# A log-sum-exp kernel: its second pass as a section with its own semaphores on the ScalarE queue, SyncE out of the branch, and a smaller sample in the range test

## The chip, the cores and the metric

The kernel runs on one core of a Trainium2 chip. The metric is the time of one execution in microseconds (us), lower is better. The profile's span, from the first to the last recorded instruction, is about 1.8 us shorter than that time in most kernels here. Engines: ACT is ScalarE, DVE is VectorE, SP is SyncE, PE is TensorE, POOL is GpSimd. A "q" after the name means the engine's sequencer (waits, branches, register loads and DMA issues, which are not counted as busy).

## The reference

The input x is 32 x 512 x 1024 float32, normally distributed: 67 MB to read, 64 KB to write.

```python
max_x = np.max(x, axis=-1, keepdims=True)
return max_x.squeeze(-1) + np.log(np.sum(np.exp(x - max_x), axis=-1))
```

## The kernel before

The first pass takes no maximum. It loads rows, takes Exp and sums, then Log. A test then decides whether every sum was in a safe range. Only if not does a second, stable pass run. On normally distributed inputs it never runs, so what matters here is what the test and the skipped branch cost.

```python
loads = ["R8 R8", "R8 R8", "R8 R8", "R7 R6 A A", ..., "T2", "T1", "A", "A"]   # 17 loads, on SyncE
ENGINES = [SP, Activation, DVE]
# ... first pass: load -> Exp on ScalarE -> sum on VectorE (R, T) or ScalarE (A) ...
nc.scalar.activation(out=res[:, EARLY:NC], in_=sumexp[:, EARLY:NC], func=AF.Ln)       # L121
nc.sync.dma_start(out=out_view, in_=res)                                              # L122

# range test: sums clamped to [1e-15, 1e15] must equal themselves (L127, L131); the last
# row is tested by the maximum of a sample of its elements (L136, L137); PE counts (L135-L141)
nc.vector.reduce_max(out=bad[:, 2:3], in_=last_row[:, 0, 0 : d // 4], axis=AX.X)      # L136
nc.vector.tensor_scalar(out=bad[:, 1:2], in0=bad[:, 2:3], scalar1=LOG_LOW, ...)       # L137
# ... three matmuls into count ...
nc.vector.tensor_scalar(out=fine, in0=count, scalar1=HIGH, scalar2=None, op0=ALU.is_lt)  # L143
all_fine = nc.values_load(fine[0:1, 0:1], engines=ENGINES, ...)                       # L144
with tc.If(all_fine < 1, preferred_fallthrough_block=False):                          # L148
    # ... second pass: loads on SyncE, max, subtract, Exp, sum, Log, store on SyncE ...
```

The framework tracks its semaphores by counting. An engine that skips the branch therefore first bumps the semaphores that the skipped instructions would have bumped. For SyncE these are four DMA semaphores.

## Time and profile before

| | value |
|---|---|
| time, median of 6 runs | 165.31 us (165.22 to 165.62) |
| DMA engines busy, 20 to 155 us | 99 to 100%, 420 to 429 GB/s |
| VectorE / ScalarE busy | 122.2 / 116.8 us |
| from the end of the last VectorE sum to the end of the span ("the tail") | 4.01 us |

The table by stages of the kernel before; its columns are the stage, its length, busy time (and count) of PE, PEld, DVE, ACT and POOL, then the granted clock, the share of the DMA engines, and GB/s.

```profile
0.00:20.00 20.00, 0.00 (x0) 0.00 (x0) 0.09 (x2) 1.28 (x1) 0.20 (x4) 1.00 0.98 410
20.00:60.00 40.00, 0.00 (x0) 0.00 (x0) 27.86 (x4) 27.90 (x4) 0.00 (x0) 1.00 0.99 424
...
140.00:155.00 15.00, 0.00 (x0) 0.00 (x0) 13.27 (x15) 14.96 (x16) 0.00 (x0) 1.00 1.00 420
155.00:161.10 6.10, 0.19 (x2) 0.09 (x2) 5.94 (x12) 5.85 (x9) 0.00 (x0) 1.00 0.56 224
161.10:164.10 3.00, 0.24 (x4) 0.14 (x4) 0.30 (x2) 0.03 (x1) 0.00 (x0) 1.00 0.10 27
```

Up to 155 us the kernel is bound by its loads. In the last 3 us no engine computes for more than a tenth of the time; what lasts there is waits and sequencer work. The timeline of the kernel before shows the way to the flag (start, duration, engine, line):

```profile
159.99 0.09 DVE L104 DVE_READ_ACCUMULATOR ring<-ring 128x1 f32 x1
...
160.66 0.41 DVE L136 TENSOR_REDUCE bad<-ring 128x1 f32<-128x256 f32 x1
...
161.15 0.35 SPq L122 DMA_DIRECT2D out_dram<-res  x1
...
161.60 0.14 DVE L143 TENSOR_SCALAR fine<-count 1x1 int32<-1x1 f32 x1 [0.33 <-PE count L141]
```

The records by source line show what the sequencers do after the flag (engine, operation, count, duration in ns as minimum/median/maximum, first and last start in us). L144 is the load of the flag, L148 the branch, L186 the closing of the program:

```profile
L144 SPq TENSOR_LOAD <-fine x1: 462/462/462, 161.8 to 161.8; - x1
L144 ACTq TENSOR_LOAD <-fine x1: 469/469/469, 161.8 to 161.8; - x1
L144 DVEq TENSOR_LOAD <-fine x1: 543/543/543, 161.8 to 161.8; - x1
...
L148 SPq EVENT_SEMAPHORE  x4: 17/17/17, 162.4 to 162.6; - x4
L148 SPq COMPARE_BRANCH  x2: 38/44/49, 162.3 to 162.7; - x2
...
L186 SPq EVENT_SEMAPHORE  x9: 17/28/28, 162.9 to 164.0; - x9
L186 SPq DRAIN  x3: 7/7/7, 163.3 to 163.6; - x3
L186 DVEq DRAIN  x2: 10/30/50, 163.2 to 163.7; - x2
```

All three engines load the flag at 161.8. SyncE then has a compare, four bumps and a jump (the profile calls both branch forms COMPARE_BRANCH), and after that a list of closing waits for the program's semaphores. Its drain is later than VectorE's, and the closing barrier, which POOL gathers, waits for the last of them.

### The profile page before, as it was taken

To read this page: it belongs to the slowest core of one execution; us is meant where nothing else is said; L and a number is where in the kernel's file an instruction comes from. 1 tells how busy PE (TensorE), PEld (TensorE's weight loads), DVE (VectorE), ACT (ScalarE), POOL (GpSimd) and SP (SyncE) were. 2 spreads that over 40 slices of the span, in tenths; PEclk is the share of its full clock that TensorE was granted. 3 is DMA by queue.
4 is the path that set the end of the run, shared out by engine and by line. 5 is a ranking of instruction groups with operands and counts; after the bars stand their busy time and mean duration, and the time that the engine had idled before them with its cause. 6 is when DMAs were issued, how large, how long until landed. Compare 5 with 4: busy or idle time off the path is not lost.

```text
span 164.1 us, 205 instructions
## 1 busy us (share of the span) xinstructions
PE 0.4 (0%) x6; PEld 0.2 (0%) x6; DVE 122.2 (74%) x44; ACT 116.8 (71%) x53; POOL 0.2 (0%) x4
## 2 busy tenths in 40 slices
PE   0000000000000000000000000000000000000001
PEld 0000000000000000000000000000000000000000
DVE  0000000699959999399999995999998999979893
ACT  3000039990699708995399929999969599999992
POOL 0000000000000000000000000000000000000000
DMA  7979998997997999899999989999999999999960
GB/s 256 511 335 431 511 399 367 511 463 304 511 431 335 511 450 404 374 464 479 433 447 419 433 365 449 419 432 440 417 439 415 433 425 419 415 421 423 409 248 20
DMA packets 2594, 67.19 MB, mean 409 GB/s; under 512 B 288, under 2 KB 416, under 8 KB 800
## 3 DMA queue, kind: packets, MB, share of 16 engines
q1 hardware_dynamic: 2592, 67.18, 95.7%
q14 instruction: 2, 0.02, 0.0%
HBM read 67.11 MB, written 0.07 MB: 409 GB/s over the span
## 4 chain that ended last, share of the span: by engine, by line
DMA 64%; DVE 22%; ACT 11%; issue 1%; SPq 0%; PE 0%; DVEq 0%
DMA ring<-in_x_dram 64%; DVE sumexp L99 20%; ACT ring L92 11%; DVE ring L104 1%; SPq L72 0%; DVE bad L136 0%; DVE clamped L127 0%; PE count L140 0%; DVE bad L137 0%; DVE clamped L131 0%; DVE fine L143 0%; PE count L141 0%; DVEq L127 0%
## 5 line engine op out<-in xcount | busy, mean ns | idle before, releaser
L99 DVE TENSOR_REDUCE sumexp<-ring 128x8 f32<-128x8192 f32 (+7 forms) x20 | 116.2, 5854 | 38.2 <-ACT ring L92 38.2
L92 ACT ACTIVATE ring<-ring 128x8192 f32<-128x8192 f32 (+7 forms) x24 | 101.7, 4283 | 43.6 <-DMA ring<-in_x_dram 43.6
L90 ACT ACTIVATE ring<-ring 128x1024 f32<-128x1024 f32 x12 | 12.5, 1039 | 0.0
L104 DVE SCALAR_TENSOR_TENSOR ring<-ring 128x512 f32<-128x512 f32 x8 | 5.1, 684 | 0.0
L90 ACT ACTIVATION_READ_ACCUMULATOR ring<-ring 128x1 f32 x12 | 2.2, 186 | 0.0
L67 ACT ACT_TABLE_LOAD x1 | 1.3, 1283 | 0.7 <-PEq L175 0.7
L90 ACT ACTIVATE last_exp<-ring 128x1024 f32<-128x1024 f32 x1 | 1.0, 1005 | 0.0
L68 DVE MEMSET ones<- 128x1 f32 x1 | 0.1, 59 | 0.8 <-PEq L175 0.8
L104 DVE DVE_READ_ACCUMULATOR ring<-ring 128x1 f32 x8 | 0.7, 82 | 0.0
L135 PE MATMUL count<-far,bad 128*1 128x1 f32 x2 | 0.2, 164 | 160.8 <-DVE clamped L131 160.8
L136 DVE TENSOR_REDUCE bad<-ring 128x1 f32<-128x256 f32 x1 | 0.4, 415 | 0.0
L143 DVE TENSOR_SCALAR fine<-count 1x1 int32<-1x1 f32 x1 | 0.1, 145 | 0.3 <-PE count L141 0.3
L131 DVE SCALAR_TENSOR_TENSOR clamped<-clamped,sumexp 128x127 f32<-128x127 f32 x1 | 0.3, 290 | 0.0
L127 DVE TENSOR_SCALAR clamped<-sumexp 128x127 f32<-128x127 f32 x1 | 0.2, 227 | 0.1
L135 PEld LDWEIGHTS count<-far,bad 128*1 128x1 f32 x2 | 0.1, 80 | 160.8 <-DVE clamped L131 160.8
L119 ACT ACTIVATE res<-sumexp 128x104 f32<-128x104 f32 x1 | 0.3, 273 | 0.0
L121 ACT ACTIVATE res<-sumexp 128x24 f32<-128x24 f32 x1 | 0.2, 222 | 0.0
L140 PE MATMUL count<-far,bad 128*1 128x1 f32 x2 | 0.2, 164 | 0.3 <-DVE bad L137 0.3
L141 PE MATMUL count<-ones,sumexp 128*1 128x1 f32 x2 | 0.2, 164 | 0.0
L90 ACT ACTIVATION_READ_ACCUMULATOR last_exp<-ring 128x1 f32 x1 | 0.2, 185 | 0.0
L137 DVE TENSOR_SCALAR bad<-bad 128x1 f32<-128x1 f32 x1 | 0.2, 154 | 0.0
L141 PEld LDWEIGHTS count<-ones,sumexp 128*1 128x1 f32 x2 | 0.1, 82 | 0.0
(7 smaller groups left out, 0.6 us busy)
## 6 DMA issues: line engine op xcount, KB each, us to landing
ring<-in_x_dram SPq DMA_DIRECT2D x1, 7680.0 KB, 33.1
ring<-in_x_dram SPq DMA_DIRECT2D x1, 7168.0 KB, 30.7
ring<-in_x_dram SPq DMA_DIRECT2D x1, 5120.0 KB, 31.4
ring<-in_x_dram SPq DMA_DIRECT2D x1, 4608.0 KB, 33.7
ring<-in_x_dram SPq DMA_DIRECT2D x1, 4096.0 KB, 29.4
ring<-in_x_dram SPq DMA_DIRECT2D x2, 2048.0 KB, 32.7
ring<-in_x_dram SPq DMA_DIRECT2D x1, 3072.0 KB, 36.3
ring<-in_x_dram SPq DMA_DIRECT2D x2, 1024.0 KB, 38.8
```

The lines of the kernel that those rows point to most:

```text
L67: nc.scalar.preload_act_table_set("natural_log_exp_and_others")
L90: exp = nc.scalar.activation(out=o, in_=v, func=AF.Exp, accum_out=sums)
L92: exp = nc.scalar.activation(out=v, in_=v, func=AF.Exp)
L99: added = [nc.vector.reduce_sum(out=sums, in_=v, axis=AX.X)]
L104: nc.vector.scalar_tensor_tensor(out=lo, in0=lo, scalar=1.0, in1=ring[:, p + r, H:d], op0=ALU.mult, op1=ALU.add, accum_out=sums[:, r : r + 1],
L119: nc.scalar.activation(out=res[:, 0:EARLY], in_=sumexp[:, 0:EARLY], func=AF.Ln)
L121: nc.scalar.activation(out=res[:, EARLY:NC], in_=sumexp[:, EARLY:NC], func=AF.Ln)
L127: nc.vector.tensor_scalar(out=clamped[:, 0:LAST], in0=sumexp[:, 0:LAST], scalar1=LOW, scalar2=HIGH, op0=ALU.max, op1=ALU.min,)
L131: nc.vector.scalar_tensor_tensor(out=clamped[:, 0:LAST], in0=clamped[:, 0:LAST], scalar=0.0, in1=sumexp[:, 0:LAST], op0=ALU.bypass, op1=AL ...
L135: nc.tensor.matmul(count, lhsT=bad[:, 0:1], rhs=far, start=True, stop=False)
L136: nc.vector.reduce_max(out=bad[:, 2:3], in_=last_row[:, 0, 0 : d // 4], axis=AX.X)
L141: nc.tensor.matmul(count, lhsT=sumexp[:, LAST:NC], rhs=ones, start=False, stop=True)
```

## The change

It means to shorten that ending. The second pass becomes a critical section with two semaphores of its own, so that the framework has no bumps of DMA semaphores to make up for when the section is skipped. Its loads and store move to the ScalarE queue, and SyncE neither loads the flag nor branches. The sample of the last row shrinks from 256 to 64 elements.

```diff
-    ENGINES = [mybir.EngineType.SP, mybir.EngineType.Activation, mybir.EngineType.DVE]
+    ENGINES = [mybir.EngineType.Activation, mybir.EngineType.DVE]
...
-    nc.vector.reduce_max(out=bad[:, 2:3], in_=last_row[:, 0, 0 : d // 4], axis=AX.X)
+    nc.vector.reduce_max(out=bad[:, 2:3], in_=last_row[:, 0, 0 : d // 16], axis=AX.X)
...
     with tc.If(all_fine < 1, preferred_fallthrough_block=False):
-        for c0 in range(0, NC, RING):
-            ...
-            load(0, c0, s)
-            nc.vector.tensor_reduce(out=neg, in_=v, op=ALU.max, axis=AX.X, negate=True)
-            ...
-        nc.sync.dma_start(out=out_view, in_=res)
+        with tc.tile_critical(sync_engine=mybir.EngineType.Activation):
+            with nc.semaphore("landed") as landed, nc.semaphore("ready") as ready:
+                for c0 in range(0, NC, RING):
+                    ...
+                    nc.scalar.dma_start(out=v, in_=x_rows[:, c0 : c0 + s, :]).then_inc(landed, 16)
+                    nc.vector.wait_ge(landed, rows)
+                    nc.vector.tensor_reduce(...).then_inc(ready, 1)
+                    ... (the same steps, each waiting on and bumping these two) ...
+                nc.scalar.dma_start(out=out_view, in_=res).then_inc(landed, 16)
+                nc.scalar.wait_ge(landed, rows + 16)
```

More of the change, by code (lines that the diff above doesn't have):

```diff
@@ L148 @@
     with tc.If(all_fine < 1, preferred_fallthrough_block=False):
-        for c0 in range(0, NC, RING):
-            s = min(RING, NC - c0)
-            v = ring[:, 0:s, :]
-            neg = clamped[:, c0 : c0 + s]
-            load(0, c0, s)
-            nc.vector.tensor_reduce(out=neg, in_=v, op=ALU.max, axis=AX.X, negate=True)
-            nc.vector.tensor_add(out=v, in0=v, in1=neg[:, :, None].to_broadcast([P, s, d]))
-            nc.scalar.activation(out=v, in_=v, func=AF.Exp)
-            nc.vector.reduce_sum(out=sumexp[:, c0 : c0 + s], in_=v, axis=AX.X)
@@ L158 @@
-        nc.scalar.activation(out=res, in_=sumexp, func=AF.Ln)
-        nc.vector.tensor_sub(out=res, in0=res, in1=clamped)
-        nc.sync.dma_start(out=out_view, in_=res)
+        with tc.tile_critical(sync_engine=mybir.EngineType.Activation):
+            with nc.semaphore("landed") as landed, nc.semaphore("ready") as ready:
+                rows = 0
+                steps = 0
+                for c0 in range(0, NC, RING):
+                    s = min(RING, NC - c0)
+                    v = ring[:, 0:s, :]
+                    neg = clamped[:, c0 : c0 + s]
+                    if c0:
+                        nc.scalar.wait_ge(ready, steps)
+                    nc.scalar.dma_start(out=v, in_=x_rows[:, c0 : c0 + s, :]).then_inc(landed, 16)
+                    rows += 16
+                    nc.vector.wait_ge(landed, rows)
+                    nc.vector.tensor_reduce(
+                        out=neg, in_=v, op=ALU.max, axis=AX.X, negate=True
+                    ).then_inc(ready, 1)
+                    nc.vector.wait_ge(ready, steps + 1)
+                    nc.vector.tensor_add(
+                        out=v, in0=v, in1=neg[:, :, None].to_broadcast([P, s, d])
+                    ).then_inc(ready, 1)
+                    nc.scalar.wait_ge(ready, steps + 2)
+                    nc.scalar.activation(out=v, in_=v, func=AF.Exp).then_inc(ready, 1)
+                    nc.vector.wait_ge(ready, steps + 3)
+                    nc.vector.reduce_sum(
+                        out=sumexp[:, c0 : c0 + s], in_=v, axis=AX.X
+                    ).then_inc(ready, 1)
+                    steps += 4
+                nc.scalar.wait_ge(ready, steps)
+                nc.scalar.activation(out=res, in_=sumexp, func=AF.Ln).then_inc(ready, 1)
+                nc.vector.wait_ge(ready, steps + 1)
+                nc.vector.tensor_sub(out=res, in0=res, in1=clamped).then_inc(ready, 1)
+                nc.scalar.wait_ge(ready, steps + 2)
+                nc.scalar.dma_start(out=out_view, in_=res).then_inc(landed, 16)
+                nc.scalar.wait_ge(landed, rows + 16)
```

## The prediction

> **What bounds the kernel.** Loads. In the table by stages the DMA engines are 98 to 100% busy from 0 to 155 us, at 410 to 429 GB/s; VectorE (122.2 us) and ScalarE (116.8 us) are not full. The chain of waits is 64% load, 22% VectorE, 11% ScalarE up to about 160 us. The order listing shows no differing load, Exp or sum, so only the last 4 us can move.
>
> **The tail before** (timeline; records by line, sequencers included). The 256-element maximum (L136) runs 160.66 to 161.08, then the threshold 161.11, matmuls 161.32, `fine` 161.60 to 161.74. SyncE, ScalarE and VectorE load `fine` at 161.77 to 161.78 (462, 469, 543 ns). SyncE then compares and branches (162.30), does four semaphore bumps (162.40 to 162.63) and a jump (162.70), and begins its closing waits at 162.87, about 65 ns apart: seven, then two drains, the last at 163.39. VectorE's closing drain is at 163.17, ScalarE's at 162.87, so SyncE comes last. The output DMA was issued at 161.15 and landed at 162.70: by 162.87 that wait was over. The closing barrier lasts to 164.09. The Trainium skill ("Advanced Engine Details and Errata", Control Flow Timing) gives about 108 ns to a compare-and-branch; here SyncE's record is 49 ns, with 100 ns from its start to the next instruction.
>
> **What the change does.**
> 1. Takes SyncE's load of `fine`, compare, four bumps and jump (161.77 to 162.87) off its path. It goes straight to the closing waits; the output's landing (162.70, second wait) then holds it. After this come four waits and two drains, about 0.38 us, so the last drain is near 163.1 instead of 163.39: gain 0.2 to 0.3 us.
> 2. Shrinks the maximum from 256 to 64 elements. The 8192-element reduction costs 8.6 us, 1.05 ns each, so 415 becomes about 210 ns: `fine` and the VectorE and ScalarE branches come 0.2 us earlier, VectorE's drain near 162.97. It mostly lets VectorE get out of 1's way; the two don't add.
> 3. Adds one semaphore bump on ScalarE (about 75 ns, hidden), and more instructions in the skipped branch. The second pass never runs on these inputs, so its new queue and semaphores cost nothing directly. From VectorE's jump over it to the next drain is 0.52 us now, ScalarE's 0.37; a longer jump might add 0.1. The Trainium skill ("Runtime: NRT & Kernel Launch", Instruction fetch mechanics) says that a taken branch outside the fetched window waits for a fetch; no instruction-queue packet falls before 163.5 us here, so I expect none.
>
> **Sum.** Span 164.09 to about 163.8 us; time 165.29 to 165.0 us, range 164.65 to 165.4. Within 2%: 0.98; the tail after the last sum is 4 us (2.4%).
>
> **What would show each step.** No SyncE load of `fine` or compare in the records; SyncE's second closing wait ends just after the output lands, near 162.7. L136 near 210 ns, `fine` near 161.4. Last drain before the barrier near 163.1 on SyncE, with VectorE and ScalarE at 163.0 or earlier. Up to 160.66 us everything equal, within 0.2 us.
>
> **What would make it wrong.** VectorE's or ScalarE's longer jump becoming last (an instruction packet before 163 us, or a gap over 0.6 us to the drain), which would cancel the gain or cost a us. Output landing varying from 1.5 us, as SyncE now follows it. Load timing varying by more than the 0.3 us sought: the runs before span 0.4 us.

## The result

The median is 165.04 us (164.92 to 165.31, 6 runs) against 165.31 us. The ratio is 0.9983 with a 95% interval of 0.9970 to 0.9996. As the interval lies below 1, the kernel is faster by some 0.3 us.

The changed kernel's table by stages, same columns:

```profile
0.00:20.00 20.00, 0.00 (x0) 0.00 (x0) 0.09 (x2) 1.28 (x1) 0.20 (x4) 1.00 0.95 403
20.00:60.00 40.00, 0.00 (x0) 0.00 (x0) 27.93 (x4) 27.90 (x4) 0.00 (x0) 1.00 0.99 428
...
140.00:155.00 15.00, 0.00 (x0) 0.00 (x0) 13.27 (x14) 14.96 (x16) 0.00 (x0) 1.00 0.99 418
```

The body is as load-bound as it was. The timeline and the records by line of the changed kernel (the closing is L208 now):

```profile
159.29 0.08 DVE L104 DVE_READ_ACCUMULATOR ring<-ring 128x1 f32 x1
...
159.96 0.21 DVE L136 TENSOR_REDUCE bad<-ring 128x1 f32<-128x64 f32 x1
...
160.46 0.35 SPq L122 DMA_DIRECT2D out_dram<-res  x1
...
160.69 0.14 DVE L143 TENSOR_SCALAR fine<-count 1x1 int32<-1x1 f32 x1 [0.33 <-PE count L141]
```

```profile
L144 ACTq TENSOR_LOAD <-fine x1: 475/475/475, 160.9 to 160.9; - x1
L144 DVEq TENSOR_LOAD <-fine x1: 661/661/661, 160.9 to 160.9; - x1
...
L208 SPq EVENT_SEMAPHORE  x8: 17/28/1111, 160.9 to 163.1; - x8
L208 SPq DRAIN  x3: 7/7/7, 162.3 to 162.7; - x3
L208 DVEq DRAIN  x2: 10/32/53, 162.4 to 162.7; - x2
```

SyncE's load, compare and bumps are gone. One of its closing waits now lasts 1111 ns. The view of SyncE's waits in the changed kernel says for what (waiter, releaser, us in total, times, longest us); the kernel before has no such line:

```profile
SPq L208 <- DMA out_dram<-res: 1.1, 1, 1.1
```

**A trap.** The two profiled spans differ by 1.0 us (164.1 and 163.1), far more than the times. Most of it is not the change. The last sum ended at 160.08 before and 159.37 after: 0.70 us of difference in a part that the change does not touch. The chains of waits show where it arose. Before:

```profile
1.16 41.18 DMA ring<-in_x_dram
...
66.73 30.68 DMA ring<-in_x_dram
...
114.76 32.49 DMA ring<-in_x_dram
```

After:

```profile
1.16 41.11 DMA ring<-in_x_dram
...
66.66 30.05 DMA ring<-in_x_dram
...
114.06 32.49 DMA ring<-in_x_dram
```

One wait for a load was 0.63 us shorter. The kernel before's profiled run (165.87 us) was also slower than all six of its timed runs. So the tails have to be compared, not the spans, and both profiles be taken again.

Counted from the end of the last VectorE sum, the sequencer records read as follows (us; a worked list from the trace's records):

```
                                   before           after
flag written, VectorE              1.52 - 1.67      1.32 - 1.47
output DMA issued, SyncE           1.07             1.09
output landed                      2.62             2.64
flag loaded, SyncE                 1.69 - 2.15      -
flag loaded, ScalarE               1.70 - 2.17      1.50 - 1.97
flag loaded, VectorE               1.70 - 2.25      1.50 - 2.16
compare, bumps, jump, SyncE        2.22 - 2.66      -
SyncE's first closing wait         2.80             1.49
SyncE's last drain                 3.310            2.999
VectorE's drain ends               3.138            3.059
POOL gathers the closing barrier   3.343            3.094
end of the span                    4.012            3.761
```

The tail fell by 0.251 us, 4.012 less 3.761. That is the size of the measured gain (0.28 us between the means). SyncE's last drain itself moved by 0.311 us (3.310 to 2.999); VectorE's drain, which was then the later one, kept 0.06 us of this from showing.

### The profile page after: what moved, and what is told of

The parts are those of the page before. It is cut to its first block, busy times and chain, and to the rows that moved or that the text cites. A ratio compares the mean times of both kernels' runs of the same rounds, so it can differ in the third digit from the quotient of the medians. Undisturbed runs are those within 1.5% of the kernel's fastest.

```text
span 163.1 us, 198 instructions
## 1 busy us (share of the span) xinstructions
PE 0.4 (0%) x6; PEld 0.2 (0%) x6; DVE 122.0 (75%) x44; ACT 116.8 (72%) x53; POOL 0.2 (0%) x4
## 4 chain that ended last, share of the span: by engine, by line
DMA 64%; DVE 22%; ACT 12%; issue 1%; SPq 0%; PE 0%; DVEq 0%
DMA ring<-in_x_dram 64%; DVE sumexp L99 20%; ACT ring L92 12%; DVE ring L104 1%; SPq L72 0%; DVE clamped L127 0%; PE count L140 0%; DVE bad L137 0%; DVE clamped L131 0%; DVE fine L143 0%; DVE bad L136 0%; PE count L141 0%; DVEq L127 0%
```

## The experiments

Theory A is that the gather of the closing barrier comes just after the latest of three ends. The first is SyncE's: the later of its own path and the landing of the output, plus the closing waits that stand behind it. The others are VectorE's and ScalarE's drains. Rival B is that SyncE's participation in the branch as such was the cost. Rival C is that the gain is scatter of the loads. Rival D is that the branch itself is the cost.

All tails run from the end of the last VectorE sum. "Ratio" is time over that of the kernel before.

| run | SyncE's last drain | VectorE's drain ends | gather | tail | ratio (95%) |
|---|---|---|---|---|---|
| before | **3.310** | 3.138 | 3.343 | 4.012 | |
| r_before | **3.320** | 3.138 | 3.353 | 4.021 | 1.0006 (0.9988-1.0024) |
| after | 2.999 | **3.059** | 3.094 | 3.761 | 0.9983 (0.9970-0.9996) |
| r_after | 3.004 | **3.069** | 3.104 | 3.771 | 0.9986 (0.9972-1.0000) |
| r_after_2 | 3.000 | **3.065** | 3.100 | 3.767 | 0.9976 (0.9962-0.9990) |
| e1_short_max | **3.169** | 3.062 | 3.202 | 3.870 | 0.9998 (0.9984-1.0011) |
| e2_long_max | 3.008 | **3.135** | 3.170 | 3.837 | 0.9987 (0.9974-1.0001) |
| e5_section_with_sp | **3.079** | 3.061 | 3.112 | 3.780 | 0.9987 (0.9974-1.0001) |
| e7_one_element | **2.989** | 2.746 | 3.021 | 3.689 | 0.9979 (0.9965-0.9992) |
| e8_more_loads | **2.774** | 2.756 | 2.807 | 3.474 | 0.9983 (0.9969-0.9997) |
| e4_no_branch | **2.866** | 1.512 | 2.898 | 3.549 | 0.9997 (0.9983-1.0010) |
| e9_act_only | **2.937** | 1.509 | 2.969 | 3.615 | 0.9994 (0.9980-1.0007) |
| e10_dve_only | **3.000** | 2.663 | 3.033 | 3.679 | 1.0009 (0.9994-1.0024) |
| e6_fall_through | **3.098** | 2.950 | 3.131 | 3.798 | 0.9998 (0.9983-1.0014) |

SyncE's drain is given by its start and VectorE's by its end. The bold number is the later one. The gather follows it by 0.03 us in every row. ScalarE's drain was never last (it ended at 2.97 or earlier). What follows the gather takes 0.65 to 0.67 us everywhere.

### The changed kernel, and the kernel before, once more

No edit.

> The changed kernel once more, unedited. Theory A: gather at 3.05 to 3.15 after the last sum, time 0.2 to 0.3 us under the kernel before. Rival C (the gain is the scatter of the loads): the time ratio is 1.000 within 0.0005, or the moment of the last sum, not the tail, differs. In the first pair of profiles the last sum came 0.70 us earlier after the change, which theory A calls chance: here it should lie anywhere within 159.2 to 160.2.

> The changed kernel a third time, on the chip of these two. Theory A: tail 3.76 to 0.03, gather at 3.10, time 0.2 to 0.3 us under the kernel before, span to time 1.77.

> The kernel before once more, unedited, for a second profile. Theory A: from the end of the last sum the tail is 4.01 us to 0.03, gather at 3.34, whatever the loads do; the last sum anywhere within 159.2 to 160.2. Rival C: the tail itself scatters by more than 0.1 us.

The tails repeat to 0.01 us: 4.012 and 4.021 before, 3.761, 3.771 and 3.767 after. The last sums were at 160.08 and 159.62 before, and at 159.37, 159.58 and 159.75 after; these ranges overlap. Rival C falls for the tail, and is right for the other 0.70 us of the first pair of profiles. For the times, an estimate: mean spans of the timed runs less these tails put the last sum at 159.6 before and 159.65 after on the one chip, and at 159.7 and 159.65 on the other, so on average it did not move by what the time gained (spans are given to 0.1 us).

### e1: the shorter maximum alone

```diff
-    nc.vector.reduce_max(out=bad[:, 2:3], in_=last_row[:, 0, 0 : d // 4], axis=AX.X)
+    nc.vector.reduce_max(out=bad[:, 2:3], in_=last_row[:, 0, 0 : d // 16], axis=AX.X)
```

> The kernel before, with only the maximum shrunk from 256 to 64 elements; SyncE still loads fine, compares, bumps and jumps. Measured from the end of the last VectorE sum, the closing barrier was gathered at 3.34 us before and 3.09 after. Theory A (the end is the latest of SyncE's path, VectorE's path and the output landing plus SyncE's closing waits): fine comes 0.2 us earlier, SyncE's first closing wait begins at about 2.60 and is held by the landing only to 2.63, so the gather is at 3.15 to 3.19: 0.15 to 0.19 us of the 0.25 come from the shorter maximum alone. Rival B (it is SyncE leaving the branch that pays): under 0.05 us, gather at 3.30 or later.

The tail fell by 0.142 us (4.012 to 3.870). SyncE's first closing wait, here the one on the output, was over at 2.654, just after the landing at 2.637, and the other six of its list still lay behind it: SyncE's last drain fell to 3.169 and no further. The view of SyncE's waits now has the line that the kernel before lacks:

```profile
SPq L186 <- DMA out_dram<-res: 0.2, 1, 0.2
```

Expected were 0.15 to 0.19, just missed. Rival B's "under 0.05" falls. The times did not show it (ratio 0.9998, whose interval allows 0.0016 less); 0.14 us is under what five rounds resolve here, and the tail is the evidence.

### e2: the rest of the change alone

```diff
-    nc.vector.reduce_max(out=bad[:, 2:3], in_=last_row[:, 0, 0 : d // 16], axis=AX.X)
+    nc.vector.reduce_max(out=bad[:, 2:3], in_=last_row[:, 0, 0 : d // 4], axis=AX.X)
```

(from the changed kernel)

> The changed kernel with the maximum put back to 256 elements; SyncE stays out of the branch. Theory A: SyncE's last drain stays near 3.0 (landing plus 0.38) but VectorE's closing drain is at 3.09 to 3.21, so the gather is at 3.17 to 3.29: 0.05 to 0.17 us less than before, less than the whole. Rival B: gather at 3.09 to 3.12, the whole 0.25 us.

The tail was 0.175 us shorter than before. SyncE's last drain stayed at 3.008, and VectorE's drain, with the flag late again, ended it at 3.135. The parts give 0.142 and 0.175, together 0.317; the whole gives 0.251. They do not add, because each uncovers the other's path.

### e5: SyncE back in the branch, the section kept

```diff
-    ENGINES = [mybir.EngineType.Activation, mybir.EngineType.DVE]
+    ENGINES = [mybir.EngineType.SP, mybir.EngineType.Activation, mybir.EngineType.DVE]
```

(from the changed kernel)

> The changed kernel with SyncE put back among the engines that load fine and branch, so the section with its own semaphores stays and the four bumps stay away. Theory A: SyncE reaches its closing waits at about 2.3 to 2.4, before the output lands at 2.63, so its leaving is not needed: gather at 3.09 to 3.17, within 0.07 us of the changed kernel (one more closing wait, 65 ns). Rival B: SyncE's load, compare and jump cost what they show, about 0.2 us, gather at 3.25 or later.

The tail was 3.780, within 0.02 us of the changed kernel. The records of the branch and the wait on the output in this kernel:

```profile
L148 SPq COMPARE_BRANCH  x2: 37/43/49, 161.5 to 161.6; - x2
...
L208 SPq EVENT_SEMAPHORE  x8: 17/28/354, 161.8 to 163.2; - x8
```

SyncE loads the flag, compares and jumps, and still begins its wait on the output 354 ns before that wait ends (at 2.649, with the landing at 2.627). With the flag early and the four bumps gone, its presence in the branch is hidden. Rival B falls: "SyncE takes no part" is worth at most 0.02 us by itself.

The list of closing waits also changed, which is easily overlooked. In the traces six waits stand behind the one on the output in the kernel before and in e1, five in e5, four in the changed kernel. From the first of these to SyncE's last drain it took 0.443 us before and 0.308 us after. So some 0.13 of the 0.31 us by which SyncE's last drain moved came from the shorter list, and the rest from SyncE's earlier arrival. In e1, with all four bumps, SyncE's jump ended at 2.478; with the 0.13 us that followed it in the kernel before, SyncE would have been at its list at 2.61, just before the landing. So the early flag alone all but hides the bumps too, and e5's last drain is 0.09 us earlier than e1's mainly because one wait less stands behind the output.

### e7: one element instead of a maximum

```diff
-    nc.vector.reduce_max(out=bad[:, 2:3], in_=last_row[:, 0, 0 : d // 16], axis=AX.X)
-    nc.vector.tensor_scalar(
-        out=bad[:, 1:2], in0=bad[:, 2:3], scalar1=LOG_LOW, scalar2=None, op0=ALU.is_lt
-    )
+    nc.vector.tensor_scalar(
+        out=bad[:, 1:2], in0=last_row[:, 0, 0:1], scalar1=LOG_LOW, scalar2=None, op0=ALU.is_lt
+    )
```

(the three matmuls were also reordered, so that the count of the clamped sums comes last)

> The changed kernel with the maximum taken out: one element of the last row is compared with the threshold (a stricter test, still safe), and the flag count adds the long chain last. The flag comes 0.25 to 0.4 us earlier. Theory A: SyncE, held by the landing, now ends it alone, last drain at 3.00, gather at 3.03 to 3.05, tail 3.71: 0.05 us less than the changed kernel and no more. Rival B' (the flag's chain sets the end): tail down by the full 0.25 to 0.4, to under 3.55.

The flag came 0.195 us earlier (1.125 against 1.320), less than the 0.25 to 0.4 expected (the source has the comparison before the clamp's check, but in the trace it runs behind it and still stands in the chain), but the tail fell by only 0.07 us, to 3.689. SyncE's last drain stayed at 2.989. Rival B' falls. The flag's chain is off the critical path from here on; the landing of the output and SyncE's list set the end.

### e8: the output's wait last in SyncE's list

```diff
-        "R8 R8", "R8 R8", "R8 R8", "R7 R6 A A", "R6 R5 A A A", "R5 R4 A", "R5 R4", "R5 T3",
+        "R8", "R8", "R8", "R8", "R8", "R8", "R7", "R6 A A", "R6", "R5 A A A", "R5", "R4 A", "R5 R4", "R5 T3",
```

(from e7; the eight DMA semaphores are used in turn, so six more loads put the output on the last one)

> The kernel of the one-element test with six of the early loads split in two (17 loads become 23), which puts the output on the last of the eight DMA semaphores in SyncE's closing waits: one pair behind it none, four pairs stand before it. Theory A: the landing at 2.66 is followed by two drains alone, last drain at about 2.80, gather at 2.83, tail near 3.50: 0.19 us less than with the output waited for second. VectorE's drain (2.70 to 2.75) is then nearly as late, so no more. If the closing waits behind the landing cost nothing (rival E), the tail stays at 3.69. The splitting may move the last sum either way; that is read apart from the tail. Time, if the loads are no worse: 0.45 to 0.55 us under the kernel before.

The tail fell by 0.215 us more, to 3.474, the shortest complete kernel here. In e7 SyncE reached the wait on the output at once and had four more behind it; here it does all the others first, one of them a wait for VectorE:

```profile
SPq L207 <- DMA out_dram<-res: 0.5, 1, 0.5
SPq L207 <- DVEq L147: 0.4, 1, 0.4
```

Rival E falls: the four closing waits behind the landing cost about 63 ns each in e7 (59 to 68, start to start), and without them the last drain follows the landing 0.226 us sooner (0.139 us after it, not 0.365). The time did not follow (median 165.28 us; ratio 0.9983): 0.45 to 0.55 us under the kernel before were expected if the loads were no worse, and the means differ by 0.25. The last sum came later: the five timed runs had a mean span of 163.5 us, and that less the tail leaves about 160.0, against 163.4 less 3.77, about 159.6, for the changed kernel on the same chip (an estimate from spans given to 0.1 us and one profile each). Why the split loads ended later was not tested.

### e4: no branch at all

```diff
-    all_fine = nc.values_load(...)
-    with tc.If(all_fine < 1, preferred_fallthrough_block=False):
-        ... the whole second pass ...
```

(right on these inputs, not in general)

> The changed kernel with the load of fine, the test and the second pass taken out (the flag is still computed; right on these inputs, not in general). A floor: nothing is left after the flag on ScalarE and VectorE. Theory A: SyncE's closing waits after the landing still end it, with two waits fewer behind the landing: gather at about 2.97, tail 3.63 to 3.67, only 0.1 to 0.15 us below the changed kernel. Rival D (the branch itself still costs what its records last, 1.1 to 1.5 us): tail under 3.2.

The tail was 3.549, against 3.63 to 3.67 expected: SyncE's last drain came at 2.866, 0.133 us before the changed kernel's 2.999, with two closing waits behind the output instead of four, as theory A has it. The expectation seems to have taken the two waits off the changed kernel's gather, which VectorE had set, and not off SyncE's own drain. So a complete removal of the branch shortens the tail by only 0.21 us, though on VectorE 1.5 us pass from the start of the flag's load to the drain. Rival D's "under 3.2" falls.

But the time did not fall with it. In the changed kernel's runs 1.73 to 1.82 us lie between span and time; here it was 2.16 to 2.21 us in all five runs. So without the branch 0.21 us were saved in the tail and about 0.4 us added behind the span. The trace of the changed kernel has a packet on the instruction queue at 162.93 us, before its span ends at 163.135, and one at 163.27, after it; here there is one, at 164.39, after the end.

### e9 and e10: a branch on one engine

```diff
-    ENGINES = [mybir.EngineType.Activation, mybir.EngineType.DVE]
+    ENGINES = [mybir.EngineType.Activation]          # e10: DVE alone
...
-        with tc.tile_critical(...): ... the whole second pass ...
+        nc.scalar.activation(out=res, in_=sumexp, func=AF.Ln)   # e10: one VectorE subtraction
```

(right on these inputs, no valid second pass)

> The changed kernel with a branch on ScalarE alone around one instruction (right on these inputs, no valid second pass). Two questions. Without the branch the span fell 0.22 us but 2.18 us instead of 1.77 passed from span to time, and its instruction packets came after the end (164.4) rather than before it. If a jump by some engine is what brings those packets early, the 1.77 returns here, with packets before the end, and time is about 0.2 us under the changed kernel; if it is VectorE's jump or the larger program, 2.18 stays. And ScalarE jumps over 3 instructions instead of 27: if distance costs, its 0.37 us between jump and drain shrinks; if any taken jump costs that, it stays. Tail about 3.60, set by SyncE.

> The same as the run with the branch on ScalarE alone, but on VectorE alone, again around one instruction (right on these inputs, no valid second pass). If VectorE's jump is what brings the instruction packets early, 1.77 us pass from span to time; if 2.17 stay, as with ScalarE's branch alone, it is not a branch on one engine, and program size is left as a candidate. VectorE jumps over 2 instructions instead of 20: if distance costs, its 0.52 us between jump and drain shrinks; if any taken jump costs that, VectorE's drain stays at 3.01 and the tail is 3.76 to 3.81.

The gap from span to time stayed at 2.16 to 2.19 us with ScalarE's branch alone and was 1.98 to 2.16 us with VectorE's. Neither brings 1.77 us back, so a jump by ScalarE alone or by VectorE alone is not enough. Nor is an early packet: e9 has its one instruction packet at 162.97 us, before its span ends at 163.39, and the long gap all the same, while e10 has two after the end. Both programs are also shorter than the changed one. What sets the gap is open.

On jumps: ScalarE took 0.37 us from the end of its jump to its drain whether it passed 3 instructions (e9), 7 (before) or 27 (after). VectorE took 0.52 us over 15 (before) or 20 (after), but 0.16 us over 2 (e10). (The counts are those of the built programs.) Why is open.

### e6: the second pass as the fall-through

```diff
-    with tc.If(all_fine < 1, preferred_fallthrough_block=False):
+    with tc.If(all_fine < 1, preferred_fallthrough_block=True):
```

> The changed kernel with the second pass as the block that falls through, so the usual way is a far taken compare-and-branch and then a jump to the next instruction. It asks what the 0.52 us (VectorE) and 0.37 us (ScalarE) between the last jump and the drain are. If every taken jump costs that: they stay, and as much is added between compare and bump, VectorE's drain at about 3.4, tail near 4.15. If distance costs it: the gap moves ahead of the bump, drain and tail unchanged, 3.77. If the gap is the drain's own: nothing moves at all, tail 3.77 and compare to bump still 0.1 us.

The jump's cost moved and did not double: VectorE took 0.52 us from its compare to its bump, ScalarE 0.38 us, and from bump to drain about 0.1 us. The trace holds one branch record for each engine, so the jump to the next instruction is not there, and the run cannot tell what such a short jump would cost. SyncE had to wait for VectorE's late bump (a record of 131 ns), which put the tail at 3.798, 0.03 to 0.04 us above the changed kernel. The time's ratio of 0.9998 is not told apart from that of the changed kernel.

### A version that beats both?

By tail, e7 and e8 beat the changed kernel. By time none is told apart from it: differences of means to the kernel before on the same chip were -0.24 and -0.35 us for repeats of the changed kernel, -0.30 for e7, -0.25 for e8.

## Why the prediction was right

- **The sum.** 165.0 us was forecast, within 2%; 165.04 was measured. The tail fell by 0.25 us in the profiles, inside the forecast 0.2 to 0.3. The forecast range, 164.65 to 165.4, also holds the time before (165.31), so the time alone could hardly have refuted it; the records of the tail are what bear it out. There was some luck: SyncE's last drain moved by 0.31 us, more than forecast, and VectorE, later than forecast, took the surplus back.
- **"SyncE comes last" before.** Right: 3.310 against VectorE's 3.138, in both profiles.
- **Step 1, SyncE goes straight to the closing waits and the landing holds it, "about 0.38 us" follow.** Right: a wait of 1111 ns on the output, landing at 2.635, last drain at 2.999, 0.36 us later. What the prediction lumped together, e5 and e2 took apart: SyncE's load, compare and jump are hidden once the bumps are gone and the flag is early, and in e1 the early flag all but hid the bumps as well. Leaving the branch was not needed. The "four waits" after the landing, six before, are a part of the gain that the prediction counted without naming it.
- **Step 2, "415 becomes about 210 ns", "the two don't add".** Right: 215 ns, flag 0.20 us earlier, and 0.142 + 0.175 against 0.251.
- **"VectorE's drain near 162.97".** Off. On the clock of the profile before it would have been at 163.085 (3.006 after the last sum). VectorE's load of the flag took 661 ns, not 543 as before, and ate 0.12 us of the 0.20. So VectorE, not SyncE, was last after the change, by 0.06 us. The three profiles of the changed kernel and e1, e5, e6 and e10, which all load the flag 1.50 us after the last sum, have 661 to 671 ns. Those that load it at 1.31 to 1.32 or at 1.70 have 539 to 546. Why is open.
- **Step 3, a longer jump "might add 0.1", no fetch.** It added nothing: 0.52 and 0.37 us as before, and in the changed kernel no instruction packet came before 162.9 us.
- **"Everything equal, within 0.2 us" up to the last sum.** Wrong for the first pair of profiles (0.70 us). The load scatter, which the prediction named as a danger from the 0.4 us range of times, was under-sized. It did not spoil the forecast of the time, probably because the six runs of each kernel average over it.

## What to carry to other kernels

When a tuned kernel ends in flags, branches and a closing barrier, list the end of each engine's path and the landing of the last output; only the latest counts, and gains on different paths did not add here. Look behind the last landing: waits that stand there (63 ns each here) add to the end unless they can be put before it, as in e8, while an engine that reaches the same list before the landing has its branch for nothing, as in e5. To compare ends, align the traces at the last common instruction, since the load scatter here (up to 0.70 us) was larger than the effect sought (0.25), and check the time too, since a shorter span (without the branch) was not a shorter time.

## What the Trainium skill lacked or had wrong

- "Advanced Engine Details and Errata", Control Flow Timing, gives about 51 ns to a branch-always and 108 ns to a compare-and-branch. The compares that did not jump come near (79 to 100 ns from start to the next instruction), and the jumps' own records last 37 to 51 ns. But from a jump's end to the next instruction it took 0.13 us more on SyncE, 0.37 on ScalarE and 0.52 on VectorE, and 0.16 on VectorE over a block of two instructions.
- "Runtime: NRT & Kernel Launch", Instruction fetch mechanics, names one cost of a taken branch, a fetch by DMA when the target is outside the pages already fetched. The 0.37 and 0.52 us above came, in the changed kernel, with no packet on the instruction queue until 162.9 us, when both jumps were over, so they are a cost that the section does not name.
- "DMA: Bandwidth & Descriptors", Latency and other measured facts, gives a `tensor_load` floor of about 600 ns. One value loaded (here from a tile, `fine`) to SyncE or ScalarE took 462 to 504 ns, to VectorE 539 to 671 ns.
- No page has the price of SyncE's closing waits: 58 to 72 ns each, start to start, with their conditions already met.
- No page says that time outside the span depends on the program: about 1.77 us from span to time with the full branch, 2.18 us without. Where the instruction packets fall does not settle it (e9).
